# A hybrid attention, state space and recurrence block: half-array matmuls issued alternating between the two halves

## The chip, the cores and the metric

The kernel runs on one core of a Trainium2 chip. The metric is the device time of one execution in microseconds. TensorE (PE in the rows) multiplies, VectorE (DVE), ScalarE (ACT) and GpSimd (POOL) do the elementwise work, and the matmul results lie in eight banks of PSUM, from which VectorE and ScalarE read them.

## The reference

The input is 1024 tokens of 1024 channels, all in float32. The program computes two blocks one after the other.

The first block normalises its input, projects it with one wide matrix, and runs two branches. One is windowed attention: 8 heads of 64 channels in two groups that share keys and values, blocks of 128 queries against up to 384 keys, with a bias by relative position. The other is a bidirectional state space scan: 32 groups of 16 channels with 64 complex states each.

```
scores = einsum('bnqhgd,bnkhd->bnhgqk', q, kw) * HEAD_DIM ** -0.5      # attention
_, xs  = lax.associative_scan(_scan_op, (a_el, bu), reverse=(d == 1))  # x_t = a x_(t-1) + b u_t
y      = y + einsum(real(xs), c_re[d]) - einsum(imag(xs), c_im[d])
```

The second block holds a bidirectional recurrence over 8 heads with a 64 x 64 state per head, a short convolution beside it, and a mixture of 16 experts of which each takes its 128 best tokens.

```
sa = einsum('bhvk,bhk->bhv', s, a_t)
s  = s * w_t + sa b_t^T + v_t k_t^T
y  = einsum('bhvk,bhk->bhv', s, r_t)
```

## The kernel before

Everything is one program in four stages. `phase_a` computes attention and the scan in four quarters of 8 groups each; the other projections of the first block (tile `prest`) are dealt out between them as filling work by `k.fill`. `merge`, `in_proj_2` and `conv` follow, then `rwkv` (the recurrence), then `moe`. The build orders the instructions of every engine itself with a model of their times, so an engine's order is a mixture of several stages, and a change in one place of the source moves instructions elsewhere. Each engine runs its own list strictly in that order; semaphores join the lists.

TensorE is an array of 128 x 128. A float32 matmul appears in the trace as two records of MATMUL, each with its own load of weights; the 256 matmuls of line L1304 are 512 records. Several groups of matmuls use half of the array. Their form is written rows * columns in the rows of the trace:

- 64*128: the contraction covers 64 partitions. Attention scores (L464, tile `psc`; the key group selects the half), the scan's lag products (L705 and L706, `plag`), the scan's output products (L789, `py`), and the decay and gate products of the recurrence (L1176, `plo`). The Gram products L1253 (`pgre` and `pgro`, one tile per half) have this form as well.
- 64*64: L1304 (`py`) and L1333 (`p`); 128*64: L1305 (`py`), L1328 and L1338 (`p`). Even heads are on partitions 0 to 63, odd heads on 64 to 127, and the two halves write the two halves of the partitions of one PSUM bank.

In `gram` and in the chain of `scan` (L1253, L1328, L1333, L1338) the inner loop runs over the halves already: `for i in range(4): for par, rows, _ in PR: mm(...)`. In the five places of the change it does not. The output of the recurrence, which is off the way to the next state, reads

```
for i in range(4):
    for par, rows, _ in PR:
        o = p[rows, 64 * i:64 * i + 64]
        mm(o, s[rows, i], R[rows, c, i], start=True, stop=False)              # L1304, 64*64
        mm(o, sv[:, par, i], gr[c][:, par, i], start=False, stop=True)        # L1305, 128*64
```

so the form changes at every matmul: even 64*64, even 128*64, odd 64*64, odd 128*64. The scan's outputs run group by group: one full matmul (L786, 128*128) and four of the same half (L789). The scores run over the four heads of one key group, then over those of the other. `plo` runs four matmuls of one half, then four of the other.

What waits for these matmuls: VectorE reduces each score tile as soon as it is there (L467; the scores' PSUM pool `g` has two banks in this stage). ScalarE copies the scan's output out of PSUM (L791, `Y`; pool `sm` of two banks), which ends a quarter. In the recurrence ScalarE copies `py` into `ys` (L1310). The chain of the recurrence runs L1328, ScalarE's `xs` (L1330), L1333, the copies `SV` on VectorE (L1334) and ScalarE (L1335), L1338, and VectorE's `t` and `SV` (L1340, L1345). Ahead of each group of chunks, `inverse` works mostly on VectorE (L1416 to L1434, tile `ipr`).

Of the kernel before, what the change touches and what calls it, by code (L numbers as in the profile page):

```python
# [37 lines left out]
def constants():  # L38
# [25 lines left out]
    # shifts by blocks of 16 rows: columns s..s+128 move row r to r + 112 - s  # L64
# [26 lines left out]
    # block 1 projections, 128 columns each: k, v, q heads (0,4) (1,5) (2,6) (3,7), u, z_attn, z_ssm, the gates in pairs  # L91
# [7 lines left out]
    # rows follow the order of the heads in z_attn / attn  # L99
# [15 lines left out]
    # block 2  # L115
# [44 lines left out]
class K:  # L160
    """what all phases share"""
# [92 lines left out]
    def piece(s, src, he="act", le="pool"):  # L254
        """a piece of a weight matrix and its split in two parts that float32r carries exactly"""
# [15 lines left out]
    def proj(s, wh, wl, xh, xl, sl, kts=8, o=0, name="pj"):  # L271
        """[128, 512] = (128 columns of the piece, from o on)^T x[:, :, sl], both in two parts"""
# [9 lines left out]
    def rsqrt(s, pool, x, n):  # L282
        """1/sqrt(x), x [128, n] > 0: a first guess from the bits, then Newton's steps"""
# [17 lines left out]
def norm_T(k, pool, xs, ntile, scale, bias, hi, lo):  # L301
    """xs: token-major [128, 1024] tiles.  hi/lo [128, 8, tokens] = (x / rms(x)) * scale + bias, channel-major"""
# [30 lines left out]
def phase_a(k):  # L333
    """block 1 up to the two branches: attention, the state space scan, the projections of their gates (through DRAM)"""
# [5 lines left out]
    with ExitStack() as cx:  # L340
# [14 lines left out]
        def rest():  # L355
            """the projections that nothing waits for at once, one half at a time: u, z_attn, z_ssm, gates"""
            for i in range(28):
                wh, wl = k.piece(A["w_in"][6 + i])
                for sl in H2:
                    ps = k.proj(wh, wl, hT, lT, sl, name="prest")  # L360
                    t = ev.tile([128, 512], F32, tag="ev", bufs=2, name="ev")
                    if i < 4:
                        # step of the chunk, chunk
# [4 lines left out]
                    elif i < 12:  # L368
                        # ps (1 + tanh(ps / 2)), twice the silu
# [3 lines left out]
                    else:  # L373
                        # tanh((ps + b) / 2) = 2 sigmoid - 1
# [7 lines left out]
        def fill(n, after=None):  # L382
            """n of them, on the tensor engine not before `after`"""
# [48 lines left out]
def attention(k, at, qT, kT, vt):  # L432
    nc, tc, A = k.nc, k.tc, k.A
    ident = k.ident
    # bias by relative position, all heads: [8, 512], then one row per query
# [9 lines left out]
    # written with a pitch of 513 and read with 512, each row comes back one further to the right  # L445
# [6 lines left out]
    for n in range(8):  # L452
# [4 lines left out]
        po = k.o("po")  # L457
        for g in range(2):
            rows, hs = slice(64 * g, 64 * g + 64), slice(4 * g, 4 * g + 4)
            mx, dn, nm, es = (at.tile([128, 4], F32, tag=t, bufs=4, name=t) for t in ("mx", "dn", "nm", "es"))  # L460
            S = []
            for i in range(4):
                ps = k.g("psc")
                nc.tensor.matmul(ps[:, :W], qT[rows, i, 128 * n:128 * n + 128],  # L464
                                 kT[rows, 128 * (n - 1) + c0:128 * (n - 1) + c1], start=True, stop=True)
                sc = at.tile([128, 384], F32, tag="sc", bufs=12, name="sc")
# [1402 lines left out]
```

## Time and profile before

| | |
|---|---|
| runs, us | 2966.04, 2939.52, 2951.01 |
| median of the runs | 2951.01 us |
| profiled execution, first to last instruction | 2946.2 us |
| mean granted TensorE clock in it | 0.847 of full |
| TensorE busy | 2567.0 us (87%) |
| VectorE busy | 1823.2 us (62%) |
| ScalarE busy | 1224.6 us (42%) |
| GpSimd busy | 1184.0 us (40%) |

The profile gives no time of its own for the profiled execution beside this span; the median of the runs lies 4.8 us above it. Attention fills about 100 to 390 us of the span, the scan's quarters 440 to 780 us, the recurrence (L1304 and L1305) 1593 to 2043 us, and the experts run from 2260 us on. The chain of waits that ended last covers only the closing norm from 2912 us on, so the tables by stage are what tells which engine bounds a stretch. The matmuls' ends are modelled, and a busy time is the union of such spans; two matmuls that run side by side show as two records with nearly the same start.

### The profile page before, as it was taken

To read this page: it belongs to the slowest core of one execution; us is meant where nothing else is said; L and a number is where in the kernel's file an instruction comes from. 1 tells how busy PE (TensorE), PEld (TensorE's weight loads), DVE (VectorE), ACT (ScalarE), POOL (GpSimd) and SP (SyncE) were. 2 spreads that over 40 slices of the span, in tenths; PEclk is the share of its full clock that TensorE was granted. 3 is DMA by queue.
4 is the path that set the end of the run, shared out by engine and by line. 5 is a ranking of instruction groups with operands and counts; after the bars stand their busy time and mean duration, and the time that the engine had idled before them with its cause. 6 is when DMAs were issued, how large, how long until landed. Compare 5 with 4: busy or idle time off the path is not lost. (4 is left out here: it accounts for less than half of the span.)

```text
span 2946.2 us, 40181 instructions
## 1 busy us (share of the span) xinstructions
PE 2567.0 (87%) x15518; PEld 2104.5 (71%) x15518; DVE 1823.2 (62%) x2635; ACT 1224.6 (42%) x2062; POOL 1184.0 (40%) x923
## 2 busy tenths in 40 slices
PE   5699988889689977999985999899886999999983
PEld 4577777777568976888775788777675787777772
DVE  7065636765323364235759847743675899999985
ACT  3133421222232143336286466432242666666662
POOL 5111123432344245446367355452321455444442
PEclk8879997888689988999975566559986999999997
DMA  4444330111154433443122122145553899999994
GB/s 172 72 159 156 109 93 29 43 51 47 65 179 137 145 113 117 153 139 101 39 76 65 39 59 58 45 131 169 183 217 140 338 367 355 327 334 329 337 322 143
DMA packets 203195, 453.27 MB, mean 154 GB/s; under 512 B 23423, under 2 KB 122815, under 8 KB 178428
## 3 DMA queue, kind: packets, MB, share of 16 engines
q1 hardware_dynamic: 186780, 401.55, 39.9%
q0 software_dynamic: 6240, 21.10, 2.8%
q10 hardware_dynamic: 9984, 28.05, 2.4%
q8 instruction: 122, 2.00, 0.3%
q14 instruction: 69, 0.57, 0.1%
HBM read 370.03 MB, written 71.97 MB: 150 GB/s over the span
## 5 line engine op out<-in xcount | busy, mean ns | idle before, releaser
L269 POOL TENSOR_TENSOR wlo<-raw,whi 128x1024 fp32r<-128x1024 f32 (+1 forms) x135 | 452.4, 3353 | 743.0 <-ACT whi L266 703.1
L266 ACT ACTIVATE whi<-raw 128x2048 fp32r<-128x2048 f32 (+1 forms) x279 | 455.9, 1649 | 405.5 <-PE prest L278 87.4
L269 DVE TENSOR_TENSOR wlo<-raw,whi 128x2048 fp32r<-128x2048 f32 x144 | 452.4, 3171 | 49.6 <-ACT whi L266 49.5
L277 PE MATMUL prest<-hTh,whi 128*128 128x512 f32 x448 | 186.4, 416 | 4.4 <-ACT ev L376 4.4
L278 PE MATMUL prest<-hTl,whi 128*128 128x512 f32 x448 | 181.8, 406 | 0.0
L279 PE MATMUL prest<-hTh,wlo 128*128 128x512 f32 x448 | 181.4, 405 | 0.0
L1777 PE MATMUL pg<-wlo,xth 128*128 128x512 f32 x256 | 108.4, 423 | 28.7 <-POOL wlo L269 25.5
L857 DVE SCALAR_TENSOR_TENSOR ac<-raw,sc,ac 128x1024 f32<-128x1024 f32 x64 | 97.3, 1532 | 32.9 <-DMA raw<-in_ada_w 24.5
L1778 PE MATMUL pg<-whi,xtl 128*128 128x512 f32 x256 | 106.4, 415 | 2.5 <-DVE xtl L1765 2.5
L277 PEld LDWEIGHTS prest<-hTh,whi 128*128 128x128 f32 x448 | 89.6, 200 | 25.0 <-ACT ev L376 5.3
L1776 PE MATMUL pg<-whi,xth 128*128 128x512 f32 x256 | 107.1, 419 | 0.0
L1777 PE MATMUL pd<-wlo,hth 128*128 128x512 f32 x256 | 101.4, 396 | 5.0 <-DVE wlo L269 4.6
L1304 PE MATMUL py<-ZR,S 64*64 64x64 f32 x512 | 104.0, 296 | 1.1 <-issue 0.6
L789 PE MATMUL py<-Wo,XS 64*128 64x128 f32 x256 | 63.1, 442 | 47.5 <-DVE XS L777 47.5
L1305 PE MATMUL py<-GR,SV 128*64 128x64 f32 x512 | 104.0, 297 | 0.0
L279 PEld LDWEIGHTS prest<-hTh,wlo 128*128 128x128 f32 x448 | 88.5, 198 | 19.8
L278 PEld LDWEIGHTS prest<-hTl,whi 128*128 128x128 f32 x448 | 89.1, 199 | 18.1
L1777 PE MATMUL pu<-wlo,xth 128*128 128x512 f32 x256 | 100.9, 394 | 0.0
L1778 PE MATMUL pu<-whi,xtl 128*128 128x512 f32 x256 | 100.3, 392 | 0.0
L1776 PE MATMUL pu<-whi,xth 128*128 128x512 f32 x256 | 100.1, 391 | 0.0
L1778 PE MATMUL pd<-whi,htl 128*128 128x512 f32 x256 | 99.9, 390 | 0.0
L1776 PE MATMUL pd<-whi,hth 128*128 128x512 f32 x256 | 92.3, 393 | 2.5 <-ACT whi L266 2.5
(573 smaller groups left out, 7090.3 us busy)
## 6 DMA issues: line engine op xcount, KB each, us to landing
raw<-in_w_g SPq DMA_DIRECT2D x64, 1024.0 KB, 8.3
raw<-in_w_u SPq DMA_DIRECT2D x64, 1024.0 KB, 7.3
raw<-in_w_d SPq DMA_DIRECT2D x64, 1024.0 KB, 7.8
raw<-in_w_in SPq DMA_DIRECT2D x69, 512.0 KB, 4.2
raw<-in_ada_w SPq DMA_DIRECT2D x48, 512.0 KB, 3.9
x<-in_x SPq DMA_DIRECT2D x16, 512.0 KB, 6.8
d_g<-ev SPq DMA_DIRECT2D x32, 256.0 KB, 2.5
gt<-d_g SPq DMA_DIRECT2D x16, 512.0 KB, 4.5
```

The lines of the kernel that those rows point to most:

```text
L266: nc.scalar.activation(hi, src, AF.Copy)
L269: (nc.gpsimd if le == "pool" else nc.vector).tensor_tensor(lo, src, hi.bitcast(F32), op=OP.subtract)
L277: mm(ps, wh[:, c], xh[:, kt, sl], start=kt == 0, stop=False)
L278: mm(ps, wh[:, c], xl[:, kt, sl], start=False, stop=False)
L279: mm(ps, wl[:, c], xh[:, kt, sl], start=False, stop=kt == kts - 1)
L789: last = nc.tensor.matmul(o_, XS[rows, 4 * d + gp, ri, d:d + 128], Wo[rows, d, ri, gp], start=False, stop=d == 1 and ri == 1)
L857: nc.vector.scalar_tensor_tensor(ac, raw, sc[:, 8 * w + p:8 * w + p + 1], ac, op0=OP.mult, op1=OP.add)
L1304: mm(o, s[rows, i], R[rows, c, i], start=True, stop=False)
L1305: mm(o, sv[:, par, i], gr[c][:, par, i], start=False, stop=True)
L1776: mm(o, h[:, kt], wh[:, c], start=kt == 0, stop=False)
L1777: mm(o, h[:, kt], wl[:, c], start=False, stop=False)
L1778: mm(o, l[:, kt], wh[:, c], start=False, stop=kt == 7)
```

## The change

Five loops are written so that a matmul of one half is followed by one of the other half. No matmul is added or removed (11,824 before and after), and no shape changes.

- `attention`: the loop over the two key groups moves inside the loop over the four heads. Both score tiles are taken from the pool of two before the two matmuls, and all eight scores of a block of queries now come before the exponentials of the first group.
- `ssm_quarter`, lag products: the order inside a pair of groups is (re, even), (re, odd), (im, even), (im, odd) in place of (re, even), (im, even), (re, odd), (im, odd).
- `ssm_quarter`, outputs: two tiles, `pye` and `pyo`, are filled at once; per pair of groups two full matmuls, then four times even, odd. Both copies to `Y` come after all 40 matmuls.
- `rwkv.prep`: `plw` and `pla` are taken together, and their matmuls alternate; the `tanh` of both follow.
- `rwkv.scan.output`: even 64*64, odd 64*64, even 128*64, odd 128*64.

Comments and docstrings are removed as well, which moves later line numbers: L1304 and L1305 become L1308 and L1310, L786 and L789 become L788 and L794, L464 becomes L465, L1176 becomes L1180.

```diff
@@ attention
-        for g in range(2):
-            rows, hs = slice(64 * g, 64 * g + 64), slice(4 * g, 4 * g + 4)
-            mx, dn, nm, es = (at.tile([128, 4], F32, tag=t, bufs=4, name=t) for t in ("mx", "dn", "nm", "es"))
-            S = []
-            for i in range(4):
-                ps = k.g("psc")
-                nc.tensor.matmul(ps[:, :W], qT[rows, i, 128 * n:128 * n + 128], kT[rows, ...], start=True, stop=True)
+        MX = [at.tile([128, 4], F32, tag="mx", bufs=4, name="mx") for _ in range(2)]
+        SC = [[], []]
+        for i in range(4):
+            pss = [k.g("psc") for _ in range(2)]
+            for g in range(2):
+                rows = slice(64 * g, 64 * g + 64)
+                nc.tensor.matmul(pss[g][:, :W], qT[rows, i, 128 * n:128 * n + 128], kT[rows, ...], start=True, stop=True)
+            for g in range(2):
...
+                nc.vector.tensor_tensor_reduce(sc[:, :W], pss[g][:, :W], bt[:, 4 * g + i, c0:c1], ...)
@@ ssm_quarter, lag products
-        for g in range(8):
-            nc.tensor.matmul(o_, V[rows, d, 0, gp], cre[rows, ix], start=True, stop=False)
-            nc.tensor.matmul(o_, V[rows, d, 1, gp], ncim[rows, ix], start=False, stop=True)
+        for gp in range(4):
+            ix = 16 * d + 4 * qt + gp
+            for ri, cx_ in enumerate((cre, ncim)):
+                for e in range(2):
+                    rows, b_ = (slice(64 * e, 64 * e + 64), 512 * e + (d * 4 + gp) * 16)
+                    nc.tensor.matmul(pk[:, b_:b_ + 16], V[rows, d, ri, gp], cx_[rows, ix], start=ri == 0, stop=ri == 1)
@@ ssm_quarter, outputs
-    for hf in range(2):
-        ps = k.sm("py")
-        for g4 in range(4):
-            nc.tensor.matmul(o_, UT[:, g], WI[:, g]..., start=True, stop=False)
-            for d in range(2):
-                for ri in range(2):
-                    last = nc.tensor.matmul(o_, XS[rows, 4 * d + gp, ri, d:d + 128], Wo[rows, d, ri, gp], start=False, ...)
-        nc.scalar.activation(Y...[:, hf::2], ps..., AF.Copy)
+    pys = (k.sm("pye"), k.sm("pyo"))
+    for gp in range(4):
+        for e in range(2):
+            nc.tensor.matmul(pys[e][:, o_], UT[:, 2 * gp + e], WI[:, 2 * gp + e]..., start=True, stop=False)
+        for d in range(2):
+            for ri in range(2):
+                for e in range(2):
+                    last = nc.tensor.matmul(pys[e][:, o_], XS[rows, 4 * d + gp, ri, d:d + 128], Wo[rows, d, ri, gp], ...)
+    for e in range(2):
+        nc.scalar.activation(Y...[:, e::2], pys[e]..., AF.Copy)
@@ rwkv.prep
-        for q, (rw, o, bias) in enumerate(((EV, th, "w0"), (OD, aa, "a0"))):
-            ps = k.g("plo")
-            for i in range(4):
-                mm(z, k.lora[rw, d, 128 * i:128 * i + 128], x, start=True, stop=True)
-            for i in range(4):
-                act(o[:, i], z, AF.Tanh, scale=0.5, bias=k.h(bias, 4 * d + i))
+        halves = ((EV, th, "w0", k.g("plw")), (OD, aa, "a0", k.g("pla")))
+        for i in range(4):
+            for rw, _, _, ps in halves:
+                mm(ps[:, 128 * i:128 * i + 128], k.lora[rw, d, 128 * i:128 * i + 128], x, start=True, stop=True)
+        for rw, o, bias, ps in halves:
+            for i in range(4):
+                act(o[:, i], ps[:, 128 * i:128 * i + 128], AF.Tanh, scale=0.5, bias=k.h(bias, 4 * d + i))
@@ rwkv.scan.output
             for i in range(4):
+                o = slice(64 * i, 64 * i + 64)
                 for par, rows, _ in PR:
-                    o = p[rows, 64 * i:64 * i + 64]
-                    mm(o, s[rows, i], R[rows, c, i], start=True, stop=False)
-                    mm(o, sv[:, par, i], gr[c][:, par, i], start=False, stop=True)
+                    mm(p[rows, o], s[rows, i], R[rows, c, i], start=True, stop=False)
+                for par, rows, _ in PR:
+                    mm(p[rows, o], sv[:, par, i], gr[c][:, par, i], start=False, stop=True)
```

TensorE's list in the recurrence, before: the outputs `py` of one step, in which each row is one matmul.

```order
L1304 MATMUL py<-ZR,S 64x64
L1305 MATMUL py<-GR,SV 64x64
L1304 MATMUL py<-ZR,S 64x64
L1305 MATMUL py<-GR,SV 64x64
L1304 MATMUL py<-ZR,S 64x64
```

The same place in the changed program, with a piece of the decay products (`pla`), of the transposes (`pvt`) and of the chain (`p`) between the outputs of two steps.

```order
L1308 MATMUL py<-ZR,S 64x64 x2
L1310 MATMUL py<-GR,SV 64x64 x2
L1180 MATMUL pla<-wa,lora 128x128 x4
L1239 MATMUL pvt<-cst,v 128x128 x4
L1308 MATMUL py<-ZR,S 64x64 x2
L1310 MATMUL py<-GR,SV 64x64 x2
```

Each line now stands twice in a row, once for the even and once for the odd heads, so the form changes after every second matmul. Over the whole program 451 of the 512 output matmuls are followed by another output matmul of the other half.

TensorE's list at the end of a quarter of the scan, before: `py` group by group, then filling work.

```order
L786 MATMUL py<-WI,UT 128x128
L789 MATMUL py<-Wo,XS 128x128 x4
L786 MATMUL py<-WI,UT 128x128
L789 MATMUL py<-Wo,XS 128x128 x4
L277 MATMUL prest<-hTh,whi 128x512
```

The same place now, with `pye` for the even and `pyo` for the odd group.

```order
L788 MATMUL pye<-WI,UT 128x128
L788 MATMUL pyo<-WI,UT 128x128
L794 MATMUL pye<-Wo,XS 128x128
L794 MATMUL pyo<-Wo,XS 128x128
L794 MATMUL pye<-Wo,XS 128x128
L794 MATMUL pyo<-Wo,XS 128x128
L794 MATMUL pye<-Wo,XS 128x128
L794 MATMUL pyo<-Wo,XS 128x128
L794 MATMUL pye<-Wo,XS 128x128
L794 MATMUL pyo<-Wo,XS 128x128
L277 MATMUL prest<-hTh,whi 128x512
```

Two groups share one block of half-array matmuls, and the filling work still comes after them. The scores are adjacent in 22 pairs of 32; elsewhere other work stands between the two halves. Of the 160 decay products 89 are now followed by the other half, 18 before.

## Rows read from the trace of the kernel before

**Rows 1.** Groups by shape: line, tiles, form, count | busy us, mean ns | idle before.
```profile
L1305 PE MATMUL py<-GR,SV 128*64 128x64 f32 x512 | 104.0, 297 | 0.0
L1304 PE MATMUL py<-ZR,S 64*64 64x64 f32 x512 | 104.0, 296 | 1.1 <-issue 0.6 <-POOL ZR L1261 0.5
...
L789 PE MATMUL py<-Wo,XS 64*128 64x128 f32 x256 | 63.1, 442 | 47.5 <-DVE XS L777 47.5
...
L464 PE MATMUL psc<-kT,qT 64*128 64x384 f32 x96 | 41.2, 576 | 5.4 <-DVE mx L467 5.4
```

**Rows 2.** Timeline of TensorE, recurrence outputs: start us, us, line, tiles, form, records.
```profile
1719.69 0.47 PE L1304 MATMUL py<-ZR,S 64*64 64x64 f32 x2
1720.10 0.47 PE L1305 MATMUL py<-GR,SV 128*64 128x64 f32 x2
```

**Rows 3.** Timeline of TensorE, two matmuls of both halves, then another form, twice.
```profile
1503.83 0.48 PE L1333 MATMUL p<-xs,TT 64*64 64x64 f32 x4
1504.24 2.07 PE L1253 MATMUL pgre<-ZR,BK 64*128 64x128 f32 x8
...
1831.04 0.48 PE L1328 MATMUL p<-SV,ZR 128*64 128x64 f32 x4
1831.45 0.47 PE L1304 MATMUL py<-ZR,S 64*64 64x64 f32 x2
```

**Rows 4.** Stretches of the recurrence: us, PE PEld DVE ACT POOL busy, PEclk, DMA, GB/s.
```profile
1600.00:1700.00 100.00, 89.72 (x995) 73.70 (x994) 87.01 (x115) 55.29 (x145) 50.73 (x49) 0.59 0.15 42
1700.00:1750.00 50.00, 50.00 (x495) 41.75 (x489) 15.42 (x23) 29.30 (x81) 22.68 (x27) 0.53 0.23 67
1750.00:1950.00 200.00, 186.32 (x1810) 152.04 (x1809) 146.48 (x206) 106.37 (x288) 93.36 (x89) 0.59 0.19 55
1950.00:2050.00 100.00, 96.80 (x951) 72.85 (x951) 30.06 (x46) 26.11 (x55) 43.40 (x31) 0.78 0.54 163
```

**Rows 5.** The same stretches, tile py alone: PE, PEld, ACT, PEclk, DMA.
```profile
1600.00:1700.00 100.00, 35.44 (x190) 25.17 (x190) 2.27 (x6) 0.59 0.15 42
1700.00:1750.00 50.00, 15.84 (x87) 11.22 (x87) 0.77 (x2) 0.53 0.23 67
1750.00:1950.00 200.00, 85.84 (x476) 60.72 (x475) 5.70 (x15) 0.59 0.19 55
1950.00:2050.00 100.00, 39.39 (x273) 28.27 (x272) 3.38 (x9) 0.78 0.54 163
```

**Rows 6.** Timeline of TensorE, scan outputs of the first quarter.
```profile
506.61 0.79 PE L786 MATMUL py<-WI,UT 128*128 128x128 f32 x2
507.33 2.07 PE L789 MATMUL py<-Wo,XS 64*128 64x128 f32 x8
509.33 0.79 PE L786 MATMUL py<-WI,UT 128*128 128x128 f32 x2
```

**Rows 7.** Timeline of TensorE, Gram products of both halves in turn.
```profile
1703.26 0.42 PE L1253 MATMUL pgre<-ZR,BK 64*128 64x128 f32 x1
1703.27 0.42 PE L1253 MATMUL pgro<-ZR,BK 64*128 64x128 f32 x1
1703.47 0.42 PE L1253 MATMUL pgre<-ZR,BK 64*128 64x128 f32 x1
```

**Rows 8.** Sum over 506:523, 590:602, 673:689 and 757:778, tile py alone.
```profile
sum 66.00, PE 62.11 PEld 51.78 ACT 2.96; mean PE 15.53 PEld 12.95 ACT 0.74
```

**Rows 9.** Stretches of attention and scan, columns as in Rows 4.
```profile
250.00:385.00 135.00, 131.26 (x654) 96.99 (x653) 83.95 (x289) 52.13 (x134) 20.98 (x35) 0.99 0.39 123
450.00:800.00 350.00, 294.09 (x1572) 242.94 (x1569) 210.26 (x326) 77.38 (x118) 114.30 (x142) 0.77 0.14 46
```

**Rows 10.** Timeline of TensorE, scan lag products: the first and the last.
```profile
612.69 0.28 PE L706 MATMUL plag<-cc__2974,V 64*128 64x16 f32 x1
...
613.94 0.26 PE L706 MATMUL plag<-cc__2974,V 64*128 64x16 f32 x1
```

**Rows 11.** Groups by shape, VectorE: the reduction of a score tile.
```profile
L467 DVE CUSTOM_DVE_ANT_0 sc<-psc,bt 128x384 f32<-128x384 f32 x48 | 26.0, 551 | 31.2 <-PE psc L464 30.6
```

More of the change, by code (lines that the diff above doesn't have):

```diff
@@ L457, in attention @@
         po = k.o("po")
[L458 to L469 removed]
+        MX = [at.tile([128, 4], F32, tag="mx", bufs=4, name="mx") for _ in range(2)]
[4 more added lines that the diff above has]
+                rows = slice(64 * g, 64 * g + 64)
+                nc.tensor.matmul(pss[g][:, :W], qT[rows, i, 128 * n:128 * n + 128],
+                                 kT[rows, 128 * (n - 1) + c0:128 * (n - 1) + c1], start=True, stop=True)
+            for g in range(2):
+                sc = at.tile([128, 384], F32, tag="sc", bufs=12, name="sc")
+                nc.vector.tensor_tensor_reduce(sc[:, :W], pss[g][:, :W], bt[:, 4 * g + i, c0:c1], 1.0, -3e38, op0=OP.add,
+                                               op1=OP.max, accum_out=MX[g][:, i:i + 1])
+                SC[g].append(sc)
+        for g in range(2):
+            hs, mx, S = slice(4 * g, 4 * g + 4), MX[g], SC[g]
+            dn, nm, es = (at.tile([128, 4], F32, tag=t, bufs=4, name=t) for t in ("dn", "nm", "es"))
             nc.vector.tensor_tensor(nm, mx, sink[:, hs], op=OP.max)
@@ L699, in ssm_quarter @@
     for d in range(2):
[L700 to L703 removed]
+        for gp in range(4):
             ix = 16 * d + 4 * qt + gp
[L705 to L706 removed]
+            for ri, cx_ in enumerate((cre, ncim)):
+                for e in range(2):
+                    rows, b_ = slice(64 * e, 64 * e + 64), 512 * e + (d * 4 + gp) * 16
+                    nc.tensor.matmul(pk[:, b_:b_ + 16], V[rows, d, ri, gp], cx_[rows, ix], start=ri == 0, stop=ri == 1)
     Kt = q.tile([128, 2, 8, 16], F32, tag="Kt", name="Kt")
@@ L779, in ssm_quarter @@
     Y = q.tile([128, 8, 128], F32, tag="Y", name="Y")
-    for hf in range(2):
-        ps = k.sm("py")
-        for g4 in range(4):
-            g = 2 * g4 + hf
-            gp, rows = g // 2, slice(64 * (g % 2), 64 * (g % 2) + 64)
-            o_ = ps[:, 128 * g4:128 * g4 + 128]
-            nc.tensor.matmul(o_, UT[:, g], WI[:, g].rearrange("p j c -> p (j c)"), start=True, stop=False)
-            for d in range(2):
-                for ri in range(2):
-                    last = nc.tensor.matmul(o_, XS[rows, 4 * d + gp, ri, d:d + 128], Wo[rows, d, ri, gp], start=False,
-                                            stop=d == 1 and ri == 1)
-        nc.scalar.activation(Y.rearrange("p j (g c) -> p g j c", c=16)[:, hf::2],
-                             ps.rearrange("p (g j c) -> p g j c", g=4, j=8), AF.Copy)
+    pys = (k.sm("pye"), k.sm("pyo"))
+    for gp in range(4):
+        o_ = slice(128 * gp, 128 * gp + 128)
+        for e in range(2):
+            nc.tensor.matmul(pys[e][:, o_], UT[:, 2 * gp + e], WI[:, 2 * gp + e].rearrange("p j c -> p (j c)"), start=True,
+                             stop=False)
+        for d in range(2):
+            for ri in range(2):
+                for e in range(2):
+                    rows = slice(64 * e, 64 * e + 64)
+                    last = nc.tensor.matmul(pys[e][:, o_], XS[rows, 4 * d + gp, ri, d:d + 128], Wo[rows, d, ri, gp],
+                                            start=False, stop=d == 1 and ri == 1)
+    for e in range(2):
+        nc.scalar.activation(Y.rearrange("p j (g c) -> p g j c", c=16)[:, e::2],
+                             pys[e].rearrange("p (g j c) -> p g j c", g=4, j=8), AF.Copy)
     if qt == 0:
```

12 lines of the change are left out of this document (1 added, 11 removed).

## The prediction

> **What bounds the kernel now.** I read the page's busy shares first; TensorE leads there by far. That share is a mean over the stages, so I went on to the groups by shape, to see which of the five loops carries time. The recurrence outputs L1304 and L1305 show 104.0 us each, the scan outputs L789 63.1 us, the larger scores L464 41.2 us [rows 1]. Then the timeline, for what one matmul takes and why. Where the form changes at every matmul, L1304 starts at 1719.69 and L1305 at 1720.10: 0.41 us for one matmul, two records [rows 2]. Two matmuls of L1333, one of each half, start at 1503.83 and the next form at 1504.24; two of L1328 start at 1831.04 and the next form at 1831.45: 0.41 us each time, for two matmuls in place of one [rows 3]. That is the price on which the forecast rests. Last, the tables by stretch tell who would be next: in the recurrence VectorE is busy for 87.01 of 100 us from 1600 on, but for only 30.06 of 100 from 1950 on [rows 4].
>
> **Recurrence outputs.** Before, each of four matmuls (even 64*64, even 128*64, odd 64*64, odd 128*64) takes 0.41 us, 1.64 us together. Now the two 64*64 run as one pair (as in L1333) and the two 128*64 as another (as in L1328), each at 0.41 us: 0.82 us. The change of form after each pair remains, so a long run in one form is not the model. TensorE's time for `py` halves. L1304 and L1305 overlap at their modelled ends, so I take the union by stretch, 35.44 + 15.84 + 85.84 + 39.39 = 176.5 us [rows 5]; half is 88.3 us.
>
> What of it lies on the path? These outputs feed nothing but a copy; they cost time because they stand in TensorE's list ahead of the chain. Taken out, VectorE is late next, with its inverse and the chain's small copies. In each stretch the gain cannot exceed VectorE's idle time, and as its work comes in dependent bursts I count half of that as usable. 1600 to 1700: half of `py` is 17.7, VectorE idle 13.0, so 6.5. 1700 to 1750: half is 7.9, idle 34.6, so 7.9. 1750 to 1950: half is 42.9, idle 53.5, so 26.8. 1950 to 2050: half is 19.7, idle 69.9, so 19.7 [rows 4, 5]. The sum is 61 us. The bounds: 28 us (7.9 + 19.7, only where VectorE is busy for under a third), and 84 us (13.0 + 7.9 + 42.9 + 19.7, all idle time used).
>
> **Scan outputs.** One group starts at 506.61 with L786, its four half-array matmuls at 507.33, the next group at 509.33: 0.72 + 2.00 = 2.72 us [rows 6]. L789 has eight records there and L786 two, and 1.28 us for six more records is 0.21 us a record. The Gram products show what alternation does to this form: `pgre` at 1703.26, `pgro` at 1703.27, the next `pgre` at 1703.47, so one record of each half in 0.21 us [rows 7]. Two groups now cost 0.72 + 0.43 for two L786, then 2.00 for both halves: 3.15 us in place of 5.44, or 58%. In the four closing runs of the quarters `py` is busy for 62.1 us [rows 8], which gives 26 us. These runs wait for VectorE's states (L789: 47.5 us idle, by XS L777 [rows 1]), and filling work stands behind them. TensorE is busy for 294.09 of 350 us in this stage [rows 9], 84%; I count that share, 22 us. The bounds are 11 us, half of it, since the rest of a quarter is VectorE's chain, and 26 us. The first copy to `Y` no longer runs beside the second half's matmuls; this is in the lower bound.
>
> **Lag products: nothing.** The last of the 24 records of this run starts 1.25 us after the first, 0.05 us a record [rows 10], against 0.21 us for a pair of the wide Gram records at the lower granted level [rows 7]. A record of this form loads as many weights as a Gram record; two of them in 0.11 us means that the halves already run side by side, in the order of two and two. The Trainium skill, TensorE: Matmul & The Clock Gate, under "What overlaps and what doesn't", says that matmuls start and end strictly in order; by that rule this loop would be serial before and would gain. The 0.05 us a record speaks against it, and the measurement decides; by the rule the loop's 256 records would go from twice 0.05 to 0.05 us, 13 us, of which 84% is 11, and the forecast would be 2857 us.
>
> **Decay products: nothing counted.** 89 of 160 are followed by the other half now and 18 before, so some 35 are newly hidden; at 0.43 us (two records at 0.21) that is up to 15 us of TensorE's time, of which the share that counted in the recurrence, 61 of 88, is 10 us. Against it, two of the four banks of pool `g` are now taken at once for the same copies. I take 0, with bounds of a gain of 10 us and, the wait being as likely to eat it twice as once, a loss of 10 us.
>
> **Scores: nothing counted.** Half of 41.2 us, 21 us, is the most that this form could give back [rows 1]. But a pair now needs both banks of its pool, so it starts only when VectorE has reduced both tiles of the pair before; a reduction takes 0.551 us [rows 11]. One more reduction per pair is 32 x 0.55 = 18 us, just as much. I take 0, with bounds of -21 and +18 us.
>
> **The sum.** 61 + 22 = 83 us less than 2946.2, that is 2863 us for the profiled execution. The median of the runs lies 4.8 us above its span, so I predict 2868 us.
>
> **Rivals.**
>
> *VectorE's chain holds the recurrence.* The outputs fill gaps that the inverse leaves, and only the stretches with an idle VectorE give time: 28 + 22 = 50 us, 2901 us. For it speaks 87.01 of 100 us in the first stretch, against it that TensorE is busy for 422.8 of the 450 us in all four [rows 4]. Chance 12%.
>
> *Everything counts.* 84 + 26 + 10 + 21 = 141 us, 2810 us. For it speaks that TensorE leads in every stage concerned; against it the waits named above. Chance 8%.
>
> *The pairs of `py` do not overlap.* They accumulate into one bank, 64*64 onto 128*64, which no pair of before does in this way. Then only every second change of form goes: a serial matmul is two records in 0.41 us, and a second one behind it in the same form costs at least two records at the 0.107 us at which a half's records of half this width could follow (half of 0.21, [rows 7]). So two matmuls cost 0.62 at the least, 0.82 at the most; the middle, 0.72, gives 12% of 176.5, 21 us, of which 61 of 88 count: 15 us. With the scan's 22 that is 37 us, 2914 us. Against it, L1333 and L1328 write both halves of one bank in their pairs at 0.41 us for two [rows 3]. The Trainium skill, TensorEngine Tiling (Array Packing), under "Gotcha 1: PSUM Pressure", says that different row tiles cannot access one PSUM bank at the same time; by that rule the 64*64 pairs would be serial and this rival would hold, and the row of L1333 speaks against it. Chance 8%.
>
> *Slower: the scores stall TensorE, and its clock falls.* In attention from 250 to 385 us TensorE is busy for 131.26 of 135 us at 0.99 of full clock [rows 9]; in the recurrence, with small matmuls only, 0.53 to 0.78 was granted [rows 4]. If every pair waits for two reductions in a row and the granted level falls to half, the stretch costs up to 131 us more, and the 18 us above: 2868 + 149 = 3017 us. It decides against the gain from 45% of that on, since the forecast gains 83. Against it, filling work stands between the scores. Chance 4%.
>
> *The change does not do what it says*, because the build's order breaks the pairs up: 451 of the 512 outputs keep a neighbour of the other half, so for them it does; for the scores (22 of 32 pairs) it may not, which the zero there covers.
>
> **How the numbers follow.** The forecast's own case, 2840 to 2890 us, has 68%. About 1%, some 29 us, is what a measurement of this kernel can tell from no change. The lower end takes the gain of the outputs at 84, of the scan at 26, and 20 of the 31 us that scores and decay products might give: 2951 - 130 = 2821, and I put 2820. The upper end takes 28 and 11, with a loss of 10 at the decay products: 2951 - 29 = 2922; I put 2918, which leaves the slower rival, no change, and part of the second case outside. Faster by over 1%: the forecast, the first two rivals and half of the third, 68 + 12 + 8 + 4, less some for what I have not seen: 0.88. Slower by over 1%: 0.04. Within 1%: 0.08.
>
> **What would show it right or wrong.** After the change L1308 and L1310 should stand in the timeline as x4 groups of 0.41 us at the lower level, and their union should fall from 176.5 to about 90 us; if it stays above 150, the third rival holds. The time from the first L1338 to the last recurrence output should shrink by about 60 us; if TensorE's idle time there grows by nearly all that `py` loses, VectorE's chain held it. The closing runs of the quarters should fall from 62 to about 36 us, the lag products should not change. If attention's last score, at 385 us before, comes later by over 20 us, the scores' wait is the cause. The forecast is wrong as a whole if the recurrence is not shorter.

## The result and the profile after

The changed kernel takes 2861.56 us, median of four runs from 2855.85 to 2865.51, against 2956.64 us for the kernel before in four runs. The ratio is 0.9666 [0.9629, 0.9703]: faster, by 95 us of the medians. The two profiled executions have spans of 2946.2 and 2857.0 us, 89 us apart; these are the ones compared below.

The groups by shape of the changed kernel answer to [rows 1]; columns as there.

```profile
L1310 PE MATMUL py<-GR,SV 128*64 128x64 f32 x512 | 57.5, 291 | 0.0
L1308 PE MATMUL py<-ZR,S 64*64 64x64 f32 x512 | 53.5, 291 | 7.5 <-ACT ys L1315 5.8 <-POOL S L1352 1.4 <-issue 0.4
L465 PE MATMUL psc<-kT,qT 64*128 64x384 f32 x96 | 39.6, 600 | 7.1 <-DVE mx L469 7.1
L794 PE MATMUL pyo<-Wo,XS 64*128 64x128 f32 x128 | 29.3, 368 | 0.0
L794 PE MATMUL pye<-Wo,XS 64*128 64x128 f32 x128 | 29.3, 368 | 49.3 <-DVE XS L781 49.3
```

The recurrence outputs fell from twice 104.0 to 57.5 and 53.5 us. The scan's 63.1 us became two tiles of 29.3 us that lie beside each other, and the idle time ahead of them, 47.5 us before, stayed (49.3). The scores stand at 39.6 in place of 41.2 us.

The timeline of TensorE shows why, first in the recurrence, once at the lower granted level and once at the upper one (start, us, line, records).

```profile
1645.07 0.48 PE L1308 MATMUL py<-ZR,S 64*64 64x64 f32 x4 [0.19 <-issue]
1645.48 0.48 PE L1310 MATMUL py<-GR,SV 128*64 128x64 f32 x4
1645.89 0.48 PE L1308 MATMUL py<-ZR,S 64*64 64x64 f32 x4
...
1671.20 0.33 PE L1308 MATMUL py<-ZR,S 64*64 64x64 f32 x4
1671.46 0.34 PE L1310 MATMUL py<-GR,SV 128*64 128x64 f32 x4
```

Two matmuls, four records, from 1645.07 to 1645.48: 0.41 us for two, where [rows 2] have 0.41 us for one. Further on, at the upper level, it is 0.26 us.

The same view at the end of the scan's third quarter answers to [rows 6].

```profile
659.04 0.79 PE L788 MATMUL pye<-WI,UT 128*128 128x128 f32 x2
...
660.18 0.58 PE L794 MATMUL pye<-Wo,XS 64*128 64x128 f32 x1
660.19 0.58 PE L794 MATMUL pyo<-Wo,XS 64*128 64x128 f32 x1
...
662.19 0.62 PE L788 MATMUL pye<-WI,UT 128*128 128x128 f32 x2
...
664.05 0.49 PE L788 MATMUL pye<-WI,UT 128*128 128x128 f32 x2
```

Each even record of L794 has its odd one 0.01 us behind it. Two groups take 3.15 us (659.04 to 662.19), exactly the forecast's figure. The next two take 1.86 us (662.19 to 664.05): the granted clock went up in between. That was not in the forecast.

The table by stretch, of three stages between the first lag product and the experts' first product, before (columns as in [rows 4]); the last two rows are for tile `py` alone (us, PE, PEld and ACT busy, PEclk, DMA, GB/s) ...

```profile
440.00:774.00 334.00, 282.98 (x1571) 235.47 (x1571) 208.94 (x324) 68.09 (x105) 107.54 (x138) 0.76 0.12 41
1341.00:2044.00 703.00, 637.28 (x5946) 520.13 (x5944) 454.93 (x608) 378.53 (x1008) 363.92 (x347) 0.69 0.24 72
2044.00:2261.00 217.00, 163.43 (x817) 139.29 (x815) 136.33 (x355) 56.36 (x105) 63.52 (x41) 0.82 0.54 189
...
440.00:774.00 334.00, 80.80 (x318) 65.85 (x319) 4.18 (x7) 0.76 0.12 41
1341.00:2044.00 703.00, 176.87 (x1024) 125.66 (x1024) 11.74 (x31) 0.69 0.24 72
```

... and after; the last two rows are the tables for tile `pye` alone and tile `py` alone.

```profile
443.00:740.00 297.00, 243.54 (x1569) 203.14 (x1571) 206.76 (x324) 66.09 (x103) 110.78 (x137) 0.82 0.14 46
1307.50:1955.00 647.50, 538.97 (x5940) 444.59 (x5938) 450.32 (x604) 374.92 (x1006) 356.12 (x345) 0.72 0.26 78
1955.00:2171.00 216.00, 161.69 (x825) 136.85 (x822) 141.04 (x359) 56.78 (x107) 62.10 (x42) 0.84 0.54 191
...
443.00:740.00 297.00, 37.46 (x159) 28.50 (x160) 1.80 (x3) 0.82 0.14 46
1307.50:1955.00 647.50, 96.00 (x1024) 67.81 (x1024) 11.62 (x31) 0.72 0.26 78
```

The second stretch runs from the first decay product to the last recurrence output. The scan lost 37 us, the second stretch 55.5 us, the third nothing. Together that is 92.5; the start of the scan came 3 us later, and the remaining stages differ by less than 2 us. In the scan TensorE is busy for 39.4 us less and its idle time rose by 2.4 us only (51.0 to 53.5): nearly all counted. In the second stretch it is busy for 98.3 us less, 80.9 of them the outputs' (176.9 to 96.0), and idle for 42.8 us more (65.7 to 108.5): something else is late there now. The other 17 us are not located one by one; run e9 below, which has the decay products as before, is busy for 6.5 us more than the change in this stretch.

The waits of TensorE in the second stretch name the largest part of it (what waited and for what: us in all, times, longest), before ...

```profile
PE p L1328 <- DVE SV L1345: 7.3, 8, 2.3
...
PE p L1338 <- ACT SV L1335: 2.4, 2, 2.0
```

... and after, with the lines five further on.

```profile
PE p L1333 <- DVE SV L1350: 19.2, 17, 2.9
PE plw L1180 <- DVE GR L1267: 17.1, 4, 8.2
PE p L1343 <- ACT SV L1340: 17.0, 11, 4.9
```

The chain's matmuls wait for their own copies: 17 times in place of 8 for VectorE's `SV`, 11 times in place of 2 for ScalarE's. These two make up 26.5 of the 42.8 us. The outputs had stood in these gaps before. In the longest of the 17 waits VectorE's copy was late because VectorE was at the inverse (`ipr`):

```profile
1654.44 2.94 DVE L1432 TENSOR_TENSOR ipr<-TI 128x1024 f32<-128x1024 f32 x1
...
1657.31 1.94 DVE L1350 TENSOR_TENSOR SV<-t,PL 64x256 f32<-64x256 f32 x2
...
1658.94 0.30 PE L1333 MATMUL p<-SV,ZR 128*64 128x64 f32 x2 [2.88 <-DVE SV L1350]
```

Over all of TensorE's waits ahead of L1333 in this stretch, 27 us by the records, VectorE was at `SV` for 12 us and at other work for 14. VectorE is busy during 96.0 of the 108.5 us in which TensorE is idle in this stretch (before: 57.8 of 65.7), worked out from the overlap of the two engines' records.

### The profile page after: what moved, and what is told of

Its sections match the earlier page's. It is cut to its first block, busy times and chain, and to the rows that moved or that the text cites. A ratio compares the mean times of both kernels' runs of the same rounds, so it can differ in the third digit from the quotient of the medians.

```text
span 2857.0 us, 40191 instructions
## 1 busy us (share of the span) xinstructions
PE 2426.5 (85%) x15518; PEld 1989.9 (70%) x15518; DVE 1817.1 (64%) x2636; ACT 1219.2 (43%) x2061; POOL 1180.1 (41%) x923
## 3 DMA queue, kind: packets, MB, share of 16 engines
q1 hardware_dynamic: 186780, 401.55, 41.2%
## 5 line engine op out<-in xcount | busy, mean ns | idle before, releaser
L863 DVE SCALAR_TENSOR_TENSOR ac<-raw,sc,ac 128x1024 f32<-128x1024 f32 x64 | 95.2, 1501 | 29.3 <-DMA raw<-in_ada_w 26.3
L469 DVE CUSTOM_DVE_ANT_0 sc<-psc,bt 128x384 f32<-128x384 f32 (+1 forms) x64 | 32.6, 519 | 102.0 <-DMA bt<-d_f 52.6
L277 PE MATMUL px<-h2h,whi 128*128 128x512 f32 x224 | 88.0, 393 | 0.0
L279 PE MATMUL px<-h2h,wlo 128*128 128x512 f32 x224 | 87.6, 391 | 0.0
```

The lines of the kernel that those rows point to most:

```text
L277: mm(ps, wh[:, c], xh[:, kt, sl], start=kt == 0, stop=False)
L279: mm(ps, wl[:, c], xh[:, kt, sl], start=False, stop=kt == kts - 1)
L469: nc.vector.tensor_tensor_reduce(sc[:, :W], pss[g][:, :W], bt[:, 4 * g + i, c0:c1], 1.0, -3e38, op0=OP.add, op1=OP.max, accum_out=MX[g][:, ...
L863: nc.vector.scalar_tensor_tensor(ac, raw, sc[:, 8 * w + p:8 * w + p + 1], ac, op0=OP.mult, op1=OP.add)
```

## The experiments

Each ratio is that of a run to runs of the kernel before on the same chip. In e1 to e3, e5, e9 and e10 the edit is made to the kernel before, in the others to the changed kernel. A trace shows one execution only, and executions of one kernel differ as well: the kernel before took from 2939.52 to 2966.04 us. Attention shows this in the traces. In six of the twelve its last score starts at 384 to 387 us, in the other six (e2, e3, e4, e6, e9, e10) at 392 to 397, whatever was done to the scores. In e3, whose source is that of the kernel before up to the scan, the granted clock of this piece is 0.92, and 0.99 before [rows 9]:

```profile
250.00:395.00 145.00, 140.09 (x657) 102.86 (x656) 82.38 (x290) 53.63 (x139) 20.35 (x35) 0.92 0.37 118
```

So a few microseconds between two single traces carry no reading.

**e1, the recurrence outputs alone.**

```diff
-                for par, rows, _ in PR:
-                    mm(o, s[rows, i], R[rows, c, i], start=True, stop=False)
-                    mm(o, sv[:, par, i], gr[c][:, par, i], start=False, stop=True)
+                for par, rows, _ in PR:
+                    mm(p[rows, o], s[rows, i], R[rows, c, i], start=True, stop=False)
+                for par, rows, _ in PR:
+                    mm(p[rows, o], sv[:, par, i], gr[c][:, par, i], start=False, stop=True)
```

> The kernel before with only the recurrence outputs alternating (even, odd, even, odd). If the two halves run side by side, a pair of matmuls takes 0.41 us at the lower granted level as one did, the union of py falls from 176.5 us to about 96 us, and the time falls by 55 to 61 us, about 2898 us beside 2955 us. If VectorE's chain holds the recurrence, it falls by no more than 28 us. If this place alone carries the whole change, it falls by 90 us.

Measured 2891.19 us, 0.979 [0.976, 0.982]: 62 us less by the ratio. The table by stretch of e1, the second and third stage:

```profile
1341.00:1991.00 650.00, 545.49 (x5967) 450.78 (x5965) 462.19 (x613) 379.20 (x1012) 369.54 (x349) 0.73 0.27 81
1991.00:2191.00 200.00, 155.49 (x800) 131.60 (x798) 128.21 (x349) 54.15 (x101) 55.23 (x39) 0.83 0.55 197
```

The second stage lost 53 us, as in the whole change (55.5). The third one lost 17 us, which the whole change does not show. After its last output 800 matmul records are left in place of 817, which fits a list with some work moved ahead; but the profiled execution is also the shortest of e1's four, by 11.6 us (2878.53 against 2890.08). The two reasons are not told apart. Over all twelve traces this stretch, whose source is always the same, takes from 200 to 221 us. So a single edit is better read from its stage than from its total.

**e2, pairs within one half.** Two 64*64 of the even heads, two 128*64 of the even heads, and so on: half as many changes of form as before, as in the change, but no neighbour of the other half.

```diff
+            for par, rows, _ in PR:
+                for i0 in (0, 2):
+                    for i in (i0, i0 + 1):
+                        mm(p[rows, 64 * i:64 * i + 64], s[rows, i], R[rows, c, i], start=i == 0, stop=False)
+                    for i in (i0, i0 + 1):
+                        mm(p[rows, 64 * i:64 * i + 64], sv[:, par, i], gr[c][:, par, i], start=False, stop=i == 3)
```

> The kernel before with the recurrence outputs in pairs of one half: two 64*64 of the even heads, two 128*64 of the even heads, and so on, the first matmul of a half alone opening its PSUM bank. The number of changes of form is that of the changed kernel (8 per output instead of 16), but no two neighbours in one form are of different halves. If the gain is the halves running side by side, two matmuls take about 0.62 us at the lower granted level (0.41 for a pair of both halves), py falls to about 135 us, and the time by 25 to 30 us. If the gain is the halved number of form changes, it falls by as much as in the run with alternating outputs, 55 to 61 us.

Measured 2909.78 us, 0.986 [0.9827, 0.9892]: 41 us less, between the two expectations. Its timeline, at the lower level:

```profile
1706.47 0.69 PE L1306 MATMUL py<-GR,SV 128*64 128x64 f32 x4
1707.09 0.69 PE L1304 MATMUL py<-ZR,S 64*64 64x64 f32 x4
```

Two matmuls of one half take 0.62 us, against 0.41 for one with its change of form, and 0.41 for two of different halves. So a second matmul in the same form costs 0.21 us in the same half and nothing in the other one, and the change of form costs the other 0.20 us. Of one output's 16 matmuls, 6.56 us before, half the changes give 1.6 us back and the overlap gives 1.7 us: in TensorE's time the two reasons weigh the same. In the stage they do not: e2 has it at 662.5 us, 40 us shorter, and e1, which adds the overlap, at 650. Neither expectation had that.

**e3, the scan outputs alone.**

```diff
-    for hf in range(2):
-        ps = k.sm("py")
+    pys = (k.sm("pye"), k.sm("pyo"))
+    for gp in range(4):
...
+        for d in range(2):
+            for ri in range(2):
+                for e in range(2):
```

> The kernel before with only the scan outputs alternating (pye, pyo). The changed kernel's scan stage ends 34 us earlier, more than the 22 us forecast. If the scan outputs are all of it, the time falls by 30 to 34 us, about 2922 us beside 2955 us, and the closing runs go to the full granted clock for half of their records as in the changed kernel. If the lag products or the scores share in it, this falls by about 22 us.

Measured 2914.99 us, 0.986 [0.9825, 0.9896]: 41 us less. Its table by stretch, the scan and the stretch behind the recurrence:

```profile
449.00:743.00 294.00, 239.78 (x1567) 200.65 (x1567) 209.13 (x324) 65.53 (x102) 108.72 (x138) 0.83 0.14 46
...
2028.00:2229.00 201.00, 157.30 (x801) 133.13 (x801) 128.85 (x350) 54.48 (x102) 53.40 (x38) 0.82 0.54 193
```

The scan gave 40 us (334 to 294), at a granted 0.83 in place of 0.76: the clock rises here with this edit alone. The 16 us behind the recurrence lie within the 200 to 221 us named at e1. The profiled execution, the longest of e3's four, is only 24 us shorter than that of before: beside the 40 and the 16 gained, the scan starts 9 us later, the second stage takes 10 us more (713), and 5 and 8 us more went by between the scan and the decay products and behind the experts' first product. None of these places was edited.

**e4, both outputs grouped by form.** Four pairs of 64*64, then four pairs of 128*64; in the scan eight full matmuls, then sixteen pairs.

```diff
+            for i in range(4):
+                for par, rows, _ in PR:
+                    mm(p[rows, 64 * i:64 * i + 64], s[rows, i], R[rows, c, i], start=i == 0, stop=False)
+            for i in range(4):
+                for par, rows, _ in PR:
+                    mm(p[rows, 64 * i:64 * i + 64], sv[:, par, i], gr[c][:, par, i], start=False, stop=i == 3)
```

> The changed kernel with the outputs also grouped by form: in the recurrence all eight 64*64 of both halves in turn, then all eight 128*64; in the scan all eight full matmuls of a quarter, then the 32 half-array ones in turn. The changes of form fall from 8 to 2 per output of the recurrence and from 8 to 2 per quarter. If TensorE still bounds the recurrence, py falls from 96 to about 55 us and the time by 20 to 30 us more, to about 2835 us. If VectorE's chain bounds it by now, py falls as much, TensorE's idle time grows instead, and the time falls by under 10 us.

Measured 2846.99 us, 0.9628 [0.9592, 0.9664]: 11 us beyond the change by the ratios, whose intervals overlap. Its timeline, then the second stage:

```profile
1641.44 1.12 PE L1307 MATMUL py<-ZR,S 64*64 64x64 f32 x16 [0.19 <-issue]
1642.49 1.12 PE L1310 MATMUL py<-GR,SV 128*64 128x64 f32 x16
...
1312.00:1956.00 644.00, 508.61 (x5992) 428.49 (x5990) 455.83 (x608) 378.13 (x1012) 361.32 (x347) 0.75 0.27 80
```

Eight matmuls take 1.05 us, 0.41 + 3 x 0.21: the price list of e2 holds. But 30 us less of TensorE's time in the second stage (539.0 to 508.6) shorten it by 3.5 us only.

**e5, the other three edits alone**: scores, lag and decay products as in the change (its diff), both outputs as before.

> The kernel before with the other three edits alone: scores, lag products and decay products alternate, both outputs are issued as before. Forecast on record: these three are worth 0 together, with 31 us of gain or 28 us of loss as the bounds. By that theory the time lies within 10 us of the kernel before, attention's last score and the first lag product stay at 386 and 440 us within 3 us, and the recurrence keeps its 532 us within 10 us. Rival, the decay products are hidden: 10 us faster or more, all of it between the decay products at 1341 us and the end of the recurrence at 2044 us. Rival, the scores' two reductions per pair hold TensorE up: 10 us slower or more, all of it before 386 us.

Measured 2951.19 us in twelve runs, 0.9953 [0.9929, 0.9978]: 14 us less, 7 to 21, more than the forecast's zero, beyond the 10 us that the expectation allowed, and less than half of the forecast's bound of 31. Where it lies stays open: its profiled execution, at 2957.4 us of span, has scan, second and third stage at 335, 711 and 216.5 us, none of them shorter by more than 0.5 us. From the first decay product to the chain's first product of `SV` and `BT` (L1338 before) it takes 160 us in place of 171, the recurrence behind it 551 in place of 532, where the expectation allowed 10 us of difference: the sum did not fall, and neither rival's place for a change shows one. Attention's last score, at 385.1 us, and the first lag product, at 441.4, stayed.

**e6, the bound of a shorter output.**

```diff
-                for par, rows, _ in PR:
-                    mm(p[rows, o], sv[:, par, i], gr[c][:, par, i], start=False, stop=True)
```

> The changed kernel with the 128*64 products of the recurrence's output left out (L1310: the part of the output that comes from the chunk's own values and from the bonus rows); only the pair of 64*64 products stays. It is no version of the kernel, but the bound of what a shorter output can bring. TensorE's time in the outputs must fall from 96 us to about a third (30 to 40 us). If VectorE's chain bounds the recurrence by now, the run is no shorter than the grouped version was, at most 20 us below the changed kernel. If TensorE's list bounds it, at least 35 of the 60 us count, and the run is 35 to 60 us below the changed kernel.

Measured 2849.37 us, 0.9613 [0.9579, 0.9647], like e4. Its table by stretch and its longest wait:

```profile
1316.50:1955.00 638.50, 485.20 (x5433) 407.29 (x5431) 456.87 (x606) 376.51 (x1008) 365.41 (x346) 0.72 0.27 80
...
PE p L1330 <- DVE SV L1347: 28.7, 25, 5.1
```

With 61 us less of outputs the stage is 9 us shorter. TensorE's list no longer sets its end; the matmuls of the chain wait 25 times for VectorE's `SV`. VectorE is busy for 457 of 638.5 us, but not evenly: while TensorE is idle, 153.3 us, VectorE is busy for 135.6 of them, some 60 with the inverse and some 30 with the chain's copies and sums. That leaves 17.7 us in which both are idle. A run with less work on VectorE was not made, so that VectorE holds the stage here is argued from these overlaps, not shown.

**e7, only the recurrence outputs grouped** (the lines of e4, the scan as in the change).

> The changed kernel with only the recurrence's outputs grouped by form (four pairs of 64*64, then four pairs of 128*64), the scan's outputs as in the changed kernel. With both grouped it was 11 to 14 us below the changed kernel. If the gain is the recurrence's, it is 8 to 14 us here too, and the output's time falls from 96 to 62 us. If it was the scan's, whose groups then had two changes of form in a quarter in place of eight, this run equals the changed kernel within 4 us.

Measured 2854.47 us, 0.9648 [0.9615, 0.9681]: 5 us beyond the change, inside the intervals. The second stage takes 643.0 us, 4.5 us less, with 37.5 us less of TensorE's time (501.4), and the scan is that of the change (297 us). The expectation of 8 to 14 us was too high.

**e8, both outputs grouped, the scores as in the kernel before.**

```diff
-        for i in range(4):
-            pss = [k.g("psc") for _ in range(2)]
+        for g in range(2):
...
+            for i in range(4):
+                ps = k.g("psc")
```

> Both outputs grouped by form, lag and decay products alternating, the scores in the order of the kernel before. If the scores' alternation is worth nothing, as forecast, this equals the version grouped by form, 11 to 14 us below the changed kernel, within 4 us. If the wait for two reductions costs something that later stages hide only in part, it is 15 to 30 us below the changed kernel; if the scores' pairs gain, it is within 8 us of the changed kernel.

Measured 2832.18 us, 0.9568 [0.9536, 0.9599]: 29 us beyond the change by the ratios, and the fastest version. Its scan:

```profile
438.80:716.40 277.60, 237.07 (x1573) 202.02 (x1572) 209.02 (x326) 68.44 (x107) 109.63 (x138) 0.84 0.18 57
```

Against e4 it gains 17 us by the ratios, whose intervals just overlap. The two profiled executions, the shortest of e8's and the longest of e4's, are 29 us apart: 9 us of that lie ahead of the first lag product (438.8 against 447.7 us), where e4 has its attention at the lower clock described above, and 17 us in the scan, 277.6 us in place of 294.6, whose source is the same in both. The total lies in the range that the expectation gave to a cost of the scores' wait, but the trace puts most of the difference in the scan.

**e9, the two outputs alternating and nothing else** (the edits of e1 and e3 together).

> The kernel before with the two outputs alternating (recurrence and scan) and nothing else: scores, lag and decay products as before. If the other three edits are worth nothing, this equals the whole change, 0.967 of the time before, within 10 us; the decay stage, from its first product to the first chain product, is 171 us again in place of 160, and the recurrence after it 10 us shorter than in the change. Rival, the three edits gave the 14 us that they had alone: then this run is 10 to 18 us slower than the change (0.971 to 0.973).

Measured 2869.38 us, 0.9688 [0.9658, 0.9718], 7 us from the whole change (0.9666) and inside its interval. Its stages:

```profile
446.70:743.50 296.80, 242.92 (x1573) 203.96 (x1572) 209.01 (x324) 65.98 (x103) 108.47 (x138) 0.82 0.14 46
1311.70:1958.50 646.80, 545.49 (x5939) 450.44 (x5938) 442.56 (x604) 377.24 (x1006) 367.26 (x345) 0.72 0.26 78
```

Scan and second stage are those of the change within 1 us; up to the chain's first product of `SV` and `BT` it takes 171 us again in place of 160, and the recurrence behind it 475 in place of 487. The two outputs carry the change.

**e10, both outputs grouped and nothing else.** As e8, with lag and decay products as before too.

> The kernel before with both outputs grouped by form, as in the fastest version so far (0.957), but with lag and decay products as before too. If the fastest version owes its lead to the old order of the scores alone, this run is at 0.954 to 0.960 as well and its scan takes 278 us, first lag product to last output. If its lead is an order of the scan's instructions that the build happened on, the scan takes 290 to 297 us here and the run is at 0.961 to 0.968.

Measured 2837.2 us, 0.9582 [0.9548, 0.9616], as e8.

```profile
446.60:731.30 284.70, 234.23 (x1573) 199.04 (x1572) 206.60 (x326) 68.81 (x107) 113.04 (x138) 0.85 0.17 55
```

The total is where the first expectation put it, the scan (285 us) between the two expectations. e8 and e10 have the old order of the scores in common, and both medians beat e4's; their stages differ from each other by 7 to 11 us each way (the second one takes 637.1 us here and 648.0 in e8). But e9 has the old scores too, and it is no faster than the change. So whether the old order of the scores is worth anything stays open.

## Why the prediction was right

The time, 2861.56 us, is 6 us below the forecast's 2868 and inside its range; by the profiled executions 89 us were saved where the sum said 83.

**The price of a pair** was right to the digit: 0.41 us for two in the recurrence, 3.15 us for two groups of the scan at the lower level. The third rival, that pairs into one bank do not overlap, falls with the row at 1645.07. The Trainium skill, TensorEngine Tiling (Array Packing), under "Gotcha 1: PSUM Pressure", says that different row tiles cannot access one PSUM bank at the same time. Read as the prediction read it, that the 64*64 pairs are serial, the trace does not agree: two of different halves take 0.41 us, two of one half 0.62 (e2). The rival had priced that case too low, at 15 us: e2 shows its lower figure, 0.62 us for two, and gains 40 us in its stage.

**Recurrence outputs, 61 us forecast.** `py` fell from 176.9 to 96.0 us (88 forecast), and the stage by 55.5. That is 69% of the 80.9 us, the same share as in the forecast, 61 of 88. VectorE's idle time was a fair stand-in, since VectorE is at work in 96.0 of the 108.5 us in which TensorE now idles; that just half of it was to be counted was a choice, and that the share came out equal is luck. The sign that the prediction named came out weaker: from the first L1338 to the last output the time fell from 532 to 487 us, 45 and not 60. The other 10.5 us of the 55.5 lie ahead of it, at the decay products (171 to 160.5), where they were not expected; with the outputs alone (e1) it is 54 us, 532 to 478. TensorE's idle time in that piece grew by 39 us, under half of what `py` lost. The versions in order of their `py` time show how the share runs out:

| version | `py`, us | stage, us | TensorE idle in it, us |
|---|---|---|---|
| before | 176.9 | 703.0 | 65.7 |
| e2, pairs in one half | 129.5 | 662.5 | 88.9 |
| e9, both outputs alone | 99.3 | 646.8 | 101.3 |
| the change | 96.0 | 647.5 | 108.5 |
| e1, recurrence outputs alone | 91.8 | 650.0 | 104.5 |
| e7, grouped by form | 66.0 | 643.0 | 141.6 |
| e10, grouped by form | 65.9 | 637.1 | 122.0 |
| e8, grouped by form | 62.9 | 648.0 | 134.5 |
| e4, grouped by form | 61.6 | 644.0 | 135.4 |
| e6, one product left out | 34.9 | 638.5 | 153.3 |

The first 47 us give 40, the next 34 give 15, the last 61 give 9. The last steps are not exact: at 62 to 66 us of `py` the stage lies anywhere between 637 and 648 us. But they are small for all of them. The first rival, VectorE's chain with 28 us, is thus wrong for the change; beyond it the stage hardly follows TensorE any more, as that rival says.

**Scan outputs, 22 us forecast, 37 measured**, beyond the upper bound of 26. The path was right, the size was not: three factors of this term were too small. The four closing runs hold 62.1 us of the outputs, but the stage has 80.8 us of them; the first outputs of each quarter start among other work and I left them out. At 58% the whole would give 34 us. The outputs shrank to 42.2 us, worked out from the union of both tiles' records, 52% and not 58%, since the granted clock rose. And nearly all of it counted, not 84%: TensorE's idle time rose by 2.4 us. The bound was none, because it was taken on the same 62.1 us. (The closing runs themselves went from 62.1 to 32.6 us, by the same union, where the prediction's sign said 36.)

**The zeros.** The lag products were paired before: 24 records in 1.25 us [rows 10]. After the change a group of 22 spans 1.51 us, the last one's own 0.26 included:

```profile
594.43 1.51 PE L710 MATMUL plag<-cc__2974,V 64*128 64x16 f32 x22
```

Two steps of the prediction's argument for this zero do not hold, though the zero does. It set 0.05 us a record, at a granted clock of 1.00, beside 0.21 us for a Gram pair at 0.50; at 1.00 a pair of the scan's outputs takes 0.11 us (663.29 to 663.40), which is two lag records, so the conclusion stands. And it read a sentence of the Trainium skill as a rule by which the old order is serial. The Trainium skill, TensorE: Matmul & The Clock Gate, under "What overlaps and what doesn't", says that matmuls start and end strictly in order. But in the order even, even, odd, odd such a start, matmul by matmul, still puts the second even one beside the first odd one, and in the trace of before each record of L706 has one of L705 within 0.01 us (the first of [rows 10] starts at 612.69):

```profile
612.70 0.28 PE L705 MATMUL plag<-cc__2974,V 64*128 64x16 f32 x1
```

So the 11 us that the prediction worked out from it were no rival, and this trace does not speak against the Trainium skill. Scores and decay products: attention's last score moved from 385.8 to 386.5 us, and e9, without these edits, is within 7 us of the change. The slower rival, scores that stall TensorE, did not come: it is busy for 132.5 of 135 us at 0.97 (131.3 at 0.99 [rows 9]).

```profile
250.00:385.00 135.00, 132.51 (x672) 98.31 (x671) 77.17 (x282) 51.87 (x133) 23.08 (x36) 0.97 0.36 114
```

This rival's sum also has a slip: the gain of 83 us is used up at 83 of 149, 56%, and not 45%. What stays open is whether the three edits give nothing or the 14 us of e5. The runs do not locate them.

The recurrence came out 6 us short and the scan 15 us long; the closeness of the total is in part luck, since these errors are opposite.

## What to carry to other kernels

For half-array matmuls count two prices from the timeline: the matmul in a run of one form, and the change of form. Here they are 0.21 and 0.20 us at the lower level; alternating halves hides every second matmul, and grouping by form removes the changes, so do both where accumulation allows it. Then multiply with the share that the stage can use, and expect it to fall as soon as the chain's own waits show up among TensorE's waits. For what holds a stage, look at what the other engines do while this one is idle, not at their mean load. Take the amount of work of a term from the whole stage, not from its clearest stretch. And judge single edits by their stage and by several runs: from one profiled execution to the next, untouched stages differed here by 10 to 20 us.

## What the runs showed of the hardware

**A change of form has a price of its own**: 0.20 us at the lower granted level (0.62 for two of one half, 0.41 for one), and at the upper one about 0.14 us, since a pair with its change takes 0.26 us and four pairs of e4 take 0.61:

```profile
1954.73 0.68 PE L1307 MATMUL py<-ZR,S 64*64 64x64 f32 x16
1955.34 0.69 PE L1310 MATMUL py<-GR,SV 128*64 128x64 f32 x16
```

The Trainium skill, TensorEngine Tiling (Array Packing), under "Key Properties", says that changing the tiling mode, not just the tile, drains TensorE. The trace agrees that a change costs time and adds the figure; that it is a drain does not show in it.

**The granted clock rose where the pairs ran.** The tables of the first and the third closing run, before (tile `py`: us, PE, PEld and ACT busy, PEclk, DMA, GB/s) ...

```profile
503.00:522.70 19.70, 18.01 (x68) 15.03 (x68) 0.60 (x1) 0.50 0.02 5
...
668.00:689.50 21.50, 17.15 (x68) 14.40 (x68) 0.60 (x1) 0.58 0.01 5
```

... and after (tile `pye`, beside which `pyo` runs; then a piece of the third run, all engines):

```profile
502.00:515.80 13.80, 8.19 (x36) 6.33 (x36) 0.00 (x0) 0.63 0.03 12
...
656.00:665.80 9.80, 6.98 (x34) 5.52 (x34) 0.00 (x0) 0.83 0.01 2
...
659.00:662.50 3.50, 3.50 (x23) 3.02 (x22) 0.00 (x0) 0.00 (x0) 0.00 (x0) 0.51 0.02 5
662.50:665.00 2.50, 2.50 (x28) 2.14 (x29) 0.00 (x0) 0.00 (x0) 0.00 (x0) 1.00 0.00 0
```

The granted clock, as a share of full, is 0.50 and 0.58 before, 0.63 and 0.83 after. Before, 31 of the outputs' 320 records ran at the upper level, after it 179. e3, with this edit alone, shows 172; with the same pairs grouped by form it is 131 in e4 and 115 in e8. In the third run TensorE was busy all the time with pairs at the lower level (0.51 from 659 to 662.5), and then with pairs at full clock. Whether the pairs themselves bring the rise, or what stands around the shorter run, was not tried apart.
